# Conv 3x3 with 2x2 max pooling on one core: six row sums read odd rows from PSUM, head casts on another engine, and a new hand-written order

## Chip, cores, metric

One core of a Trainium2 chip. The metric is device microseconds of one execution. The kernel before took 104.8 us (median of 3 runs, 104.37 to 104.86).

## The reference

A batch of 16 images, 64 channels, 64x64, is convolved with 128 filters of 3x3 (padding 1), and each 2x2 block of the result is reduced to its maximum. The innermost lines are

```python
conv[b, co] += weight[co, ci, kh, kw] * x_pad[b, ci, kh:kh+h, kw:kw+w]
output[b, c, i, j] = np.max(conv[b, c, i*2:(i+1)*2, j*2:(j+1)*2])
```

with inputs and output in float32.

## The kernel before

**Tiles.** Two images stand on the 128 partitions (2 x 64 channels). Each pair of images is cut into four chunks of 16 input rows, which makes 8 x 4 = 32 steps, numbered 0 to 31. A step computes 8 pooled rows of two images. Index h (0 or 1) is the image: it uses rows 0 to 63 or 64 to 127 of TensorE, and matmuls of the two halves are issued in turn so that they run side by side. `lanes` (L251 to L259) holds products of h = 0 and h = 1 back until it has one of each, and then issues their three taps alternately; `product` is called once for each half.

**Two kinds of steps.** For a pair of output rows y0, y1 the kernel never needs the rows themselves, only their maximum, and that allows fewer products. In a K step (11 of 32) four products, PA1, PA2 (into a tile called `ta`) and PB1, PB2 (into `tb`), make y0 and y1 less a common part; the common part is PR, a product on the row sum `ks` of even and odd rows. The order is: `EV` copies `ta` to SBUF on ScalarE (L399), `MX` takes the maximum of `tb` and that copy on VectorE (L427), and PR is then added on TensorE. In a W step (21 of 32) the operands are made from the input in float32: the difference `we` of even and odd rows (step E), the differences `wd` of rows two apart (step D), and the sum `ws` of even and odd rows (step WS). P2 (on we) and P0 (on wd) go into `ta`; `SE` copies `ta` into `tb` on ScalarE (L411), P3 is added there, `EV` copies minus `ta` to SBUF (L401), `MX` takes the maximum, and P1 (on ws) is added at the end. In both kinds `OD` then copies the odd columns to SBUF on ScalarE (L431), and `CM` takes the maximum of even and odd columns on VectorE into an output tile (L437), which is stored by SyncE (SP) when both halves are done; the last step is stored half by half from the ScalarE queue and SP.

**Where the operands are made.** All E and D run on GpSimd (L332, L341) but for the E steps in `DIFF_ON_VECTOR`. A row sum WS runs on VectorE, as a plain sum of two SBUF operands (L323), or, for the steps in `SUM_BY_REDUCTION`, as a reduction over a doubled axis (L315). `on_vector` and `on_gpsimd` (L73 to L79) make a GpSimd instruction wait for the VectorE instruction marked last before it in the order; the reductions are not marked.

**PSUM.** There are eight accumulators of one bank each, handed out by the queue `free` (`take`, L222): every `ta`, every `tb` and every turned weight block takes one and gives it back.

**Head.** The weights are combined into seven blocks (D2, G0, D0, G2, GM, G1, GP): g0, g1 and g2 are casts on ScalarE (L461 to L463), D0, D2, GM and GP are made on VectorE, GS on GpSimd, u... copies one tap on GpSimd, T... turns a block on TensorE (L164), and V... (`turn_out`) copies it to `wt`. The first chunk of image pair 0 is loaded in two parts into `kfirst` and cast to bf16 in four pieces, XOa, XOb (odd rows) and XEa, XEb (even rows), on VectorE (L451). The second chunk goes to `ksecond` and is cast in two pieces, X1 and X2, on ScalarE (L458). Step 0 is multiplied in half products F.k.part (k: PA1, PA2, PB1, PB2), step 1 in G.k.part (k: P2, P0, P3), whose operands are made by Ea, Eb (VectorE) and Da, Db (GpSimd), with SEa and SEb as the halves of its seed.

**Loads.** W chunks go into three big tiles `wx` from SP (steps L and LB; LB waits for the marked VectorE instruction before it), later K chunks are cast by the GpSimd queue's DMA (LK, L95).

**Order.** Every engine works through its instructions in the order in which the string `ORDER` (L493 to L546) names the steps: one token is one call, `P2.4.1` being product P2 of step 4 for h = 1.

Of the kernel before, what the change touches and what calls it, by code (L numbers as in the profile page):

```python
# [11 lines left out]
def kernel(  # L12
# [169 lines left out]

# [126 lines left out]

    def ws(s):  # L310
# [17 lines left out]
    def we(s):  # L328
        row["we", s] = e_pool.tile([128, R, W], BF16, name="we")
        t, f = wx_rows(s)  # L330
        vector = s in DIFF_ON_VECTOR
        inst = (nc.vector if vector else nc.gpsimd).tensor_tensor(  # L332
            out=row["we", s], in0=t[:, f : f + 2 * R : 2, :], in1=t[:, f + 1 : f + 2 * R : 2, :], op=SUB
        )
        (on_vector if vector else on_gpsimd)(inst)
# [57 lines left out]
    ev, od, ot, made = {}, {}, {}, {}  # L393
# [39 lines left out]
    def colmax(s, h):  # L433
# [5 lines left out]
        made[s] = made.get(s, 0) + 1  # L439
# [3 lines left out]
        if s == N - 1:  # L443
            store = nc.scalar if made[s] == 1 else nc.sync
            store.dma_start(out=dst[:, h : h + 1], in_=src[:, h : h + 1])
        elif made[s] == 2:
            nc.sync.dma_start(out=dst, in_=src)


    def cast_rows(lo, hi):  # L450
        on_vector(nc.vector.tensor_copy(out=kx[0][:, lo:hi:2, :], in_=kfirst[:, lo:hi:2, :]))  # L451

    def cast_more(first):
# [13 lines left out]
        "GM": lambda: on_vector(nc.vector.tensor_sub(out=slots(GM), in0=gsum, in1=g1)),  # L467
        "GP": lambda: on_vector(nc.vector.tensor_add(out=slots(GP), in0=gsum, in1=g1)),
        "XOa": lambda: cast_rows(1, kmid),
        "XOb": lambda: cast_rows(kmid, khi),  # L470
        "XEa": lambda: cast_rows(0, kmid),
        "XEb": lambda: cast_rows(kmid + 1, khi),
# [11 lines left out]
        "SE": seed, "EV": evac, "MX": rowmax, "OD": odd, "CM": colmax,  # L484
    }
# [4 lines left out]
    for m in PRODUCTS:  # L490
# [7 lines left out]
        OD.0.0 OD.0.1 EV.1.0 KS.2 E.3 CM.0.1 EV.1.1 P1.1.1 D.3 CM.0.0 PR.2.1 PB1.2.0 P2.3.0 MX.1.0 PB2.2.0  # L498
        EV.2.1 P1.3.1 SE.3.1 EV.2.0 WS.3 MX.1.1 P1.1.0 SE.3.0 P0.3.0 MX.2.0 MX.2.1 EV.3.1 PR.2.0 EV.3.0 D.4
        MX.3.1 OD.2.0 PA1.5.1 OD.1.0 E.4 PA1.5.0 PA2.5.0 P3.3.0 OD.1.1 OD.2.1 L.12 L.14 PA2.5.1 OD.3.1  # L500
        P2.4.1 CM.1.1 CM.2.0 P2.4.0 CM.1.0 PA1.7.1 D.6 EV.5.0 CM.3.1 CM.2.1 MX.3.0 PA2.7.1 PB1.5.1 SE.4.0
        PA1.7.0 PA2.7.0 EV.5.1 SE.4.1 EV.7.0 PB2.5.1 P0.4.1 P0.4.0 P2.6.1 KS.7 E.6 P3.4.1 WS.4 WS.6 P1.3.0
        EV.4.0 PR.5.1 KS.5 WS.8 EV.7.1 P0.6.1 PB1.5.0 PB1.7.0 PB2.5.0 PB2.7.0 L.16 P1.4.1 EV.4.1 MX.5.1
        P3.4.0 OD.3.0 SE.6.1 MX.5.0 LK.1.0 LK.1.1 CM.3.0 MX.4.1 P3.6.1 OD.5.1 PB1.7.1 MX.7.0 PB2.7.1 PR.5.0
        OD.5.0 P2.6.0 EV.6.1 E.8 PR.7.0 MX.4.0 OD.4.1 OD.7.0 CM.5.1 D.8 P1.4.0 SE.6.0 OD.4.0 CM.5.0 E.9
        MX.6.1 CM.7.0 CM.4.0 P1.6.1 P2.8.0 CM.4.1 D.9 P2.8.1 SE.8.0 P0.6.0 P2.9.1 MX.7.1 P3.6.0 OD.6.1
        EV.6.0 P0.8.0 L.17 P3.8.0 SE.8.1 CM.6.1 PR.7.1 EV.8.0 OD.7.1 P0.8.1 MX.6.0 SE.9.1 E.11 MX.8.0 P1.6.0
        D.11 CM.7.1 P2.9.0 OD.6.0 EV.8.1 CM.6.0 WS.9 P3.8.1 P1.8.0 P0.9.1 PA1.10.1 SE.9.0 P2.11.0 OD.8.0
        L.19 L.20 P3.9.1 PA2.10.1 KS.10 EV.9.1 SE.11.0 P0.9.0 CM.8.0 E.14 P2.11.1 MX.9.1 P3.9.0 MX.8.1
        P0.11.0 EV.9.0 EV.10.1 MX.9.0 P1.9.1 D.14 E.12 P1.8.1 PA1.10.0 P3.11.0 PA2.10.0 SE.11.1 OD.9.1  # L510
        P1.9.0 P2.14.0 WS.11 CM.9.1 P0.11.1 P3.11.1 EV.11.0 EV.11.1 OD.8.1 OD.9.0 EV.10.0 P1.11.0 PA1.13.0
        PA1.13.1 MX.11.0 MX.11.1 PA2.13.1 D.12 L.22 L.23 PA2.13.0 P2.12.0 CM.8.1 CM.9.0 D.16 P1.11.1 EV.13.1
        P2.12.1 OD.11.0 SE.14.0 OD.11.1 PB1.10.1 WS.14 P0.14.0 CM.11.0 PB2.10.1 P3.14.0 CM.11.1 L.24 P0.12.0
        SE.12.1 P0.12.1 SE.12.0 P3.12.1 P3.12.0 EV.14.0 PB1.10.0 P2.14.1 WS.12 PB2.10.0 EV.13.0 MX.10.1
        EV.12.1 MX.14.0 E.16 EV.12.0 MX.12.1 PR.10.1 P1.14.0 MX.12.0 SE.14.1 OD.10.1 P1.12.0 PB1.13.1
        PA1.18.0 KS.15 KS.13 CM.10.1 P0.14.1 MX.10.0 OD.14.0 P3.14.1 CM.14.0 EV.14.1 P1.12.1 PR.10.0
        PB2.13.1 WS.16 MX.13.1 PA2.18.0 PA1.15.1 PA2.15.1 PR.13.1 OD.10.0 MX.14.1 PB1.13.0 OD.12.1 EV.18.0
        LK.2.0 P1.14.1 PB2.13.0 P2.16.0 CM.10.0 L.25 PA1.15.0 OD.12.0 EV.15.1 OD.13.1 CM.12.1 PA2.15.0
# [75 lines left out]
```

## Time and profile before

| what | value |
|---|---|
| median of three runs | 104.8 us (104.37 to 104.86) |
| span of the profiled execution | 103.4 us, granted TensorE clock 0.997 |
| TensorE (PE) busy | 96.6 us, 93% of the span, 909 matmuls |
| VectorE (DVE) busy | 91.9 us, 89% |
| ScalarE (ACT) busy | 82.1 us, 79% |
| GpSimd (POOL) busy | 75.7 us, 73% |
| bytes read and written | 17.14 MB and 8.39 MB |

The profile cuts the span into 40 equal slices of 2.6 us; each digit is the busy share of a slice in tenths.

```profile
PE   6889899999999999999999999999999999999910
DVE  1389899999999999999999999999989996979960
ACT  4545988986789997993887898987899898698820
POOL 6046969773995899998999997959997919970000
DMA  2989999999899999999847997198699232006252
```

A busy TensorE is not necessarily one at its peak, since matmuls overlap; the distance from one start to the next tells more. The other three compute engines feed it (GpSimd, VectorE) and empty its banks (ScalarE, VectorE), and idle time of theirs costs nothing by itself. The span ends with the last store.

### The profile page before, as it was taken

To read this page: it belongs to the slowest core of one execution; us is meant where nothing else is said; L and a number is where in the kernel's file an instruction comes from. 1 tells how busy PE (TensorE), PEld (TensorE's weight loads), DVE (VectorE), ACT (ScalarE), POOL (GpSimd) and SP (SyncE) were. 2 spreads that over 40 slices of the span, in tenths; PEclk is the share of its full clock that TensorE was granted. 3 is DMA by queue.
4 is the path that set the end of the run, shared out by engine and by line. 5 is a ranking of instruction groups with operands and counts; after the bars stand their busy time and mean duration, and the time that the engine had idled before them with its cause. 6 is when DMAs were issued, how large, how long until landed. Compare 5 with 4: busy or idle time off the path is not lost.

```text
span 103.4 us, 2542 instructions
## 1 busy us (share of the span) xinstructions
PE 96.6 (93%) x909; PEld 60.1 (58%) x909; DVE 91.9 (89%) x179; ACT 82.1 (79%) x181; POOL 75.7 (73%) x65
## 2 busy tenths in 40 slices
PE   6889899999999999999999999999999999999910
PEld 2366544555865565577777774556645777776500
DVE  1389899999999999999999999999989996979960
ACT  4545988986789997993887898987899898698820
POOL 6046969773995899998999997959997919970000
PEclk9999999999999999999999999999999999999998
DMA  2989999999899999999847997198699232006252
GB/s 63 265 297 283 389 319 337 384 405 270 219 212 307 304 302 292 341 356 225 175 131 210 252 381 263 51 203 271 173 158 257 80 136 101 0 13 223 74 202 102
DMA packets 13341, 23.33 MB, mean 226 GB/s; under 512 B 1040, under 2 KB 9488, under 8 KB 13328
## 3 DMA queue, kind: packets, MB, share of 16 engines
q1 hardware_dynamic: 12320, 20.68, 61.1%
q0 software_dynamic: 864, 2.36, 13.9%
q8 instruction: 7, 0.11, 0.4%
q10 hardware_dynamic: 144, 0.13, 0.4%
q14 instruction: 6, 0.05, 0.2%
HBM read 17.14 MB, written 8.39 MB: 247 GB/s over the span
## 4 chain that ended last, share of the span: by engine, by line
PE 83%; DMA 6%; DVE 5%; SPq 1%; issue 1%; DVEq 0%
PE acc L200 83%; DMA wx<-in_x_dram 6%; DVE acc L427 2%; DVE o L437 2%; DVE we L353 1%; SPq L114 0%; SPq L113 0%; SPq L109 0%; DVE ks L301 0%; DVEq L589 0%; DVEq L437 0%
## 5 line engine op out<-in xcount | busy, mean ns | idle before, releaser
L200 PEld LDWEIGHTS <-wt 64*128 64x128 bf16 x876 | 57.7, 94 | 34.1 <-issue 1.6
L341 POOL TENSOR_TENSOR wd<-wx 128x1024 bf16<-128x1024 f32 x20 | 47.1, 2360 | 7.6 <-PE acc L200 2.9
L200 PE MATMUL acc<-kx,wt 64*128 64x504 bf16 (+6 forms) x288 | 50.1, 356 | 0.4 <-DVE wt L181 0.4
L200 PE MATMUL acc<-wd,wt 64*128 64x504 bf16 (+3 forms) x264 | 50.1, 367 | 0.0
L427 DVE TENSOR_TENSOR acc<-acc,ev 128x512 f32<-128x512 f32 x64 | 42.0, 693 | 0.9 <-ACT ev L401 0.3
L200 PE MATMUL acc<-we,wt 64*128 64x512 bf16 (+2 forms) x132 | 31.9, 367 | 0.0
L200 PE MATMUL acc<-ws,wt 64*128 64x504 bf16 (+1 forms) x126 | 28.7, 377 | 0.1
L401 ACT ACTIVATE ev<-acc 128x512 f32<-128x512 f32 x42 | 25.1, 608 | 2.7 <-PE acc L200 2.3
L431 ACT COPY od<-acc 128x256 f32<-128x256 f32 x64 | 22.6, 379 | 5.8 <-PE acc L200 5.2
L437 DVE TENSOR_TENSOR o<-acc,od 128x256 f32<-128x256 f32 x64 | 24.5, 416 | 2.1 <-ACT od L431 1.9
L411 ACT COPY acc<-acc 128x512 f32<-128x512 f32 x40 | 23.0, 581 | 3.0 <-PE acc L200 1.7
L332 POOL TENSOR_TENSOR we<-wx 128x512 bf16<-128x512 f32 x16 | 20.2, 1271 | 3.4 <-DVE ws L323 2.4
L200 PE MATMUL acc<-ks,wt 64*128 64x504 bf16 (+1 forms) x66 | 16.5, 377 | 0.4 <-DVE acc L427 0.4
L315 DVE TENSOR_REDUCE ws<-wx 128x512 bf16<-128x1024 f32 x11 | 13.5, 1230 | 0.0
L399 ACT COPY ev<-acc 128x512 f32<-128x512 f32 x22 | 12.9, 595 | 0.6 <-PE acc L200 0.5
L323 DVE TENSOR_TENSOR ws<-wx 128x512 bf16<-128x512 f32 x10 | 7.0, 720 | 0.0
L301 DVE TENSOR_TENSOR ks<-kx 128x512 bf16<-128x512 bf16 x11 | 4.6, 429 | 0.4 <-ACT kx L458 0.4
L551 PE MATMUL acc<-const-bfloat16-1.0 128*128 128x512 bf16 x8 | 3.3, 589 | 0.8 <-PEq L575 0.8
L95 POOL DMA_DIRECT2D kx<-in_x_dram x6 | 3.5, 587 | 0.7 <-DVE kx L451 0.7
L151 POOL COPY wq<-wq 128x64 bf16<-128x64 bf16 x3 | 0.9, 314 | 3.2 <-ACT wq L462 2.5
L465 DVE TENSOR_TENSOR wq<-wraw 128x192 bf16<-128x192 f32 x1 | 0.5, 498 | 2.6 <-DMA wraw<-in_weight_dram 2.6
L368 POOL TENSOR_TENSOR wd<-wx 128x512 bf16<-128x512 f32 x2 | 2.5, 1260 | 0.4 <-DVE we L353 0.4
(30 smaller groups left out, 22.7 us busy)
## 6 DMA issues: line engine op xcount, KB each, us to landing
out_dram<-o SPq DMA_DIRECT2D x31, 256.0 KB, 4.7
wx<-in_x_dram SPq DMA_DIRECT2D x10, 512.0 KB, 7.8
wx<-in_x_dram SPq DMA_DIRECT2D x5, 544.0 KB, 8.7
wx<-in_x_dram SPq DMA_DIRECT2D x5, 480.0 KB, 7.7
kx<-in_x_dram POOLq DMA_DIRECT2D x2, 528.0 KB, 8.5
ksecond<-in_x_dram SPq DMA_DIRECT2D x1, 512.0 KB, 8.0
kx<-in_x_dram POOLq DMA_DIRECT2D x2, 256.0 KB, 6.7
kx<-in_x_dram POOLq DMA_DIRECT2D x1, 496.0 KB, 13.1
```

The costliest lines, as they stand in the source:

```text
L200: nc.tensor.matmul(acc[t][:, i0:i1, o0:o1], wt[lo : lo + CI, tap_of(m0, kw, h), :], rows(lo, i0, i1, c0, c1), start=start and kw == 1, sto ...
L301: nc.vector.tensor_tensor(out=row["ks", s], in0=t[:, f : f + 2 * R : 2, :], in1=t[:, f + 1 : f + 2 * R : 2, :], op=ADD)
L315: nc.vector.tensor_reduce(out=row["ws", s], in_=t[:, f : f + 2 * R, :].rearrange("p (r two) w -> p r w two", two=2), axis=mybir.AxisListTy ...
L323: nc.vector.tensor_tensor(out=row["ws", s], in0=t[:, f : f + 2 * R : 2, :], in1=t[:, f + 1 : f + 2 * R : 2, :], op=ADD)
L332: inst = (nc.vector if vector else nc.gpsimd).tensor_tensor(out=row["we", s], in0=t[:, f : f + 2 * R : 2, :], in1=t[:, f + 1 : f + 2 * R : ...
L341: nc.gpsimd.tensor_tensor(out=row["wd", s], in0=t[:, f + 1 : f + 1 + 2 * R, :], in1=t[:, f - 1 : f - 1 + 2 * R, :], op=SUB)
L399: nc.scalar.copy(out=ev[s, h], in_=acc[t])
L401: nc.scalar.mul(ev[s, h], acc[t], -1.0)
L411: nc.scalar.copy(out=acc[t], in_=acc[ta[s, h]])
L427: nc.vector.tensor_tensor(out=t, in0=t, in1=ev[s, h], op=MAX)
L431: nc.scalar.copy(out=od[s, h], in_=acc[tb[s, h]][:, :, 1::2])
L437: nc.vector.tensor_tensor(out=ot[s][:, h], in0=acc[t][:, :, 0::2], in1=od[s, h], op=MAX)
```

## The change

Six of the 21 row sums (steps 6, 8, 9, 17, 20, 24) get a new step XC: ScalarE copies the chunk's odd rows from `wx` into a free PSUM bank, and VectorE adds the even rows in SBUF to it. Where the step's difference E is on VectorE too (6 and 8), it reads the same bank. The bank goes back to `free` after the last reader. These instructions are not marked with `on_vector`. The lists of steps are changed: E of 3, 6, 8 on VectorE (before 3, 4, 6, 11), eight reductions (before eleven). XEa, XEb and XOb move from VectorE to ScalarE; of the turned blocks ScalarE copies GM and G1 (before GM, G0, G2). The pools of SBUF buffers are larger. A store is a token of its own (ST), so that SP can issue it later than directly after its CM. `ORDER` is new in every line; the new options that are empty tuples do nothing.

```diff
-    DIFF_ON_VECTOR = (3, 4, 6, 11,)
+    DIFF_ON_VECTOR = (3, 6, 8,)
-    SUM_BY_REDUCTION = (1, 3, 9, 11, 12, 14, 16, 17, 19, 20, 22,)
+    SUM_BY_REDUCTION = (1, 3, 12, 14, 16, 22, 28, 31,)
+    ODD_ROWS_IN_PSUM = (6, 8, 9, 17, 20, 24,)
+    TURNED_BY_SCALAR = ("GM", "G1",)
+    CAST_BY_SCALAR = ("XEa", "XEb", "XOb",)
...
-    d_pool = ctx.enter_context(tc.tile_pool(name="d_pool", bufs=5))
-    e_pool = ctx.enter_context(tc.tile_pool(name="e_pool", bufs=5))
-    ws_pool = ctx.enter_context(tc.tile_pool(name="ws_pool", bufs=5))
+    d_pool = ctx.enter_context(tc.tile_pool(name="d_pool", bufs=8))
+    e_pool = ctx.enter_context(tc.tile_pool(name="e_pool", bufs=7))
+    ws_pool = ctx.enter_context(tc.tile_pool(name="ws_pool", bufs=7))
...
-    ev_pool = ctx.enter_context(tc.tile_pool(name="ev_pool", bufs=7))
-    od_pool = ctx.enter_context(tc.tile_pool(name="od_pool", bufs=6))
-    o_pool = ctx.enter_context(tc.tile_pool(name="o_pool", bufs=6))
+    ev_pool = ctx.enter_context(tc.tile_pool(name="ev_pool", bufs=8))
+    od_pool = ctx.enter_context(tc.tile_pool(name="od_pool", bufs=8))
+    o_pool = ctx.enter_context(tc.tile_pool(name="o_pool", bufs=8))
...
+    def odd_rows(s):
+        t, f = wx_rows(s)
+        copied[s] = free.popleft()
+        users[s] = 2 if s in DIFF_ON_VECTOR else 1
+        nc.scalar.copy(out=acc[copied[s]], in_=t[:, f + 1 : f + 2 * R : 2, :])
+
+    def with_odd_rows(s, out, op):
+        t, f = wx_rows(s)
+        nc.vector.tensor_tensor(out=out, in0=t[:, f : f + 2 * R : 2, :], in1=acc[copied[s]], op=op)
+        users[s] -= 1
+        if users[s] == 0:
+            free.append(copied[s])
...
     def ws(s):
         row["ws", s] = ws_pool.tile([128, R, W], BF16, name="ws")
         t, f = wx_rows(s)
+        if s in ODD_ROWS_IN_PSUM:
+            with_odd_rows(s, row["ws", s], ADD)
+            return
...
-        made[s] = made.get(s, 0) + 1
+
+    def store(s, h=None):
         p, q = place[s]
         dst = out[2 * p : 2 * p + 2, :, q * R : (q + 1) * R, :].rearrange("b c h w -> c b (h w)")
         src = ot[s].rearrange("p b h w -> p b (h w)")
...
+        if h is None:
             nc.sync.dma_start(out=dst, in_=src)
+        else:
+            (nc.scalar, nc.sync)[h].dma_start(out=dst[:, h : h + 1], in_=src[:, h : h + 1])
...
+        "XC": odd_rows, "ST": store,
...
     ORDER = """
-        D0 g2 g1 TD0 TG2 g0 D2 XEa LB.3 LB.4 PR.0.1 TD2 VG2 PA1.2.1 VD0 TG0 uG1 TG1 GS F.2.0 VD2 XOa LB.6
-        LB.8 LB.9 GM VG0 F.3.0 XOb F.0.0 uGM F.1.0 VG1 F.0.1 TGM PA2.2.1 XEb LK.0.0 F.1.1 F.2.1 F.3.1 VGM GP
-        Ea KS.0 Eb EV.0.1 G.0.0 EV.0.0 G.0.1 uGP P2.3.1 SEa.0 SEa.1 SEb.1 MX.0.1 Da Db TGP SEb.0 MX.0.0 VGP
-        LK.0.1 X2 PR.0.0 G.1.0 X1 G.2.0 PB1.2.1 PB2.2.1 WS.1 G.2.1 G.1.1 L.11 P0.3.1 PA1.2.0 PA2.2.0 P3.3.1
+        g0 D2 D0 XOa g2 TD2 g1 TG0 XOb TD0 VD2 TG2 VG0 VD0 LB.3 GS GM F.0.0 uGM F.1.0 LB.9 XEb LB.4 LB.6 F.0.1
+        XEa GP F.1.1 uG1 F.2.0 EV.0.1 VG2 TGM KS.0 VGM uGP TG1 Ea F.3.0 EV.0.0 F.2.1 F.3.1 LK.0.0 VG1 G.0.0
+        SEa.0 SEa.1 Eb MX.0.1 TGP X1 G.0.1 X2 Da MX.0.0 LB.8 PR.0.1 VGP PR.0.0 PB1.2.0 PA1.2.0 SEb.0 Db WS.1
+        SEb.1 OD.0.1 OD.0.0 PA2.2.0 PA1.2.1 KS.2 CM.0.1 CM.0.0 G.1.0 E.3 G.1.1 EV.1.0 G.2.0 LK.0.1 L.11 P2.3.0
+        G.2.1 PA2.2.1 EV.1.1 MX.1.0 PB1.2.1 P2.3.1 EV.2.1 D.3 EV.2.0 MX.1.1 WS.3 L.17 PB2.2.0 PB2.2.1 SE.3.0
...
-        EV.31.1 P1.30.1 OD.29.1 P1.30.0 MX.31.1 OD.29.0 P1.31.1 CM.29.0 CM.29.1 P1.31.0 OD.30.1 CM.30.1
-        OD.30.0 OD.31.0 OD.31.1 CM.30.0 CM.31.0 CM.31.1
+        MX.30.1 P0.31.1 ST.25 P0.31.0 P3.31.1 ST.28 ST.26 P3.31.0 ST.21 EV.31.1 MX.29.0 P1.30.1 MX.31.1 ST.16
+        EV.31.0 OD.30.1 ST.27 MX.31.0 PR.29.1 PR.29.0 CM.30.1 P1.31.1 P1.31.0 ST.23 OD.29.0 CM.29.0 OD.29.1
+        OD.31.1 OD.31.0 CM.29.1 CM.31.1 CM.31.0 ST.30 ST.29 ST.31.1 ST.31.0
     """
```

Of the tokens in between, the prediction speaks of these, in the order in which they stand: after PR.2, the ScalarE queue has OD.2.1, XC.8, OD.3.0, SE.4.1; GpSimd has D.3, E.4, D.4, a kx load, D.6, a kx load, E.9, E.11, E.12, D.8, D.9, D.11, E.14, D.14, D.12, D.16; SP has LB.3, LB.9, LB.4, LB.6, LB.8, L.11, L.17, L.14, L.12, L.22, L.20, ST.2, L.25, L.16, L.23, ST.0.

More of the change, by code (lines that the diff above doesn't have):

```diff
@@ L331, in we @@
         vector = s in DIFF_ON_VECTOR
+        if vector and s in ODD_ROWS_IN_PSUM:
+            with_odd_rows(s, row["we", s], SUB)
+            return
         inst = (nc.vector if vector else nc.gpsimd).tensor_tensor(
@@ L442, in colmax, with cast_rows @@
         src = ot[s].rearrange("p b h w -> p b (h w)")
[L443 to L446, printed above, removed]
+        if h is None:
             nc.sync.dma_start(out=dst, in_=src)
-    def cast_rows(lo, hi):
-        on_vector(nc.vector.tensor_copy(out=kx[0][:, lo:hi:2, :], in_=kfirst[:, lo:hi:2, :]))
+        else:
+            (nc.scalar, nc.sync)[h].dma_start(out=dst[:, h : h + 1], in_=src[:, h : h + 1])
+    def cast_rows(n, lo, hi):
+        if n in CAST_BY_SCALAR:
+            nc.scalar.copy(out=kx[0][:, lo:hi:2, :], in_=kfirst[:, lo:hi:2, :])
+        else:
+            on_vector(nc.vector.tensor_copy(out=kx[0][:, lo:hi:2, :], in_=kfirst[:, lo:hi:2, :]))
     def cast_more(first):
@@ L466 @@
         "GS": lambda: on_gpsimd(nc.gpsimd.tensor_tensor(out=gsum, in0=g0, in1=g2, op=ADD)),
[L467 to L472, printed above, removed]
+        "GM": lambda: tap_sum("GM", GM, SUB),
+        "GP": lambda: tap_sum("GP", GP, ADD),
+        "XOa": lambda: cast_rows("XOa", 1, kmid),
+        "XOb": lambda: cast_rows("XOb", kmid, khi),
+        "XEa": lambda: cast_rows("XEa", 0, kmid),
+        "XEb": lambda: cast_rows("XEb", kmid + 1, khi),
         "X1": lambda: cast_more(0),
@@ L499 @@
[L499 to L518, printed above, removed]
```

104 lines of the change are left out of this document (68 added, 36 removed).

## The prediction

> **What bounds the kernel now.** I read the chain of waits first, then the timeline of the head and the tail, then the busy time by 5 us windows. The chain of waits (start, us, what) gives the shape of the whole:
>
> ```profile
> span 103.4 us, 2542 instructions
> 9.65 1.30 DVE acc L427 x2
> 10.99 64.95 PE acc L200 x609
> 75.96 20.42 PE acc L200 x186
> 97.73 1.74 DVE o L437 x5
> ```
>
> From 10.99 on, TensorE is the chain without a break worth naming: (64.95 + 20.42) us over 795 matmuls is 107.4 ns each. Two matmuls run side by side (the two 64-row halves), so a pair takes 0.215 us. The timeline of a quiet stretch shows one half starting at 92.31, 92.53 and 92.75, steps of 0.22: the body runs at its own pace. Taking 0.216 a pair, the starts of the trace lie later than that pace by about 0.5 us in sum between 13.02 and 97, the largest single gap 0.24 at 75.96. What a new order can win is there, in the head and in the tail:
>
> ```profile
> 9.65 1.28 DVE L427 TENSOR_TENSOR acc<-acc,ev 128x512 f32<-128x512 f32 x2
> 10.35 1.30 ACT L423 COPY acc<-acc 128x256 f32<-128x256 f32 x4 [0.47 <-ACT ev L399]
> 10.99 0.82 PE L200 MATMUL acc<-ks,wt 64*128 64x512 bf16 x6 [0.43 <-DVE acc L427]
> 11.54 1.15 ACT L458 CAST kx<-ksecond 128x512 bf16<-128x512 f32 x2
> 11.70 1.49 PE L200 MATMUL acc<-wd,wt 64*128 64x256 bf16 x24
> 13.02 1.25 PE L200 MATMUL acc<-kx,wt 64*128 64x512 bf16 x10
> ```
>
> At 10.99 the product PR.0 waited for the two row maxima MX.0 (DVE, 9.65 to 10.93); the matmuls that read the casts X1 and X2 (L458) come at 13.02, after the 24 of G.1 and G.2 on wd, so those casts hold nothing up.
>
> **The change, part by part.** Row prices:
>
> ```profile
> L315 DVE TENSOR_REDUCE ws<-wx 128x512 bf16<-128x1024 f32 x11 | 13.5, 1230 | 0.0
> L323 DVE TENSOR_TENSOR ws<-wx 128x512 bf16<-128x512 f32 x10 | 7.0, 720 | 0.0
> L427 DVE TENSOR_TENSOR acc<-acc,ev 128x512 f32<-128x512 f32 x64 | 42.0, 693 | 0.9 <-ACT ev L401 0.3
> L411 ACT COPY acc<-acc 128x512 f32<-128x512 f32 x40 | 23.0, 581 | 3.0 <-PE acc L200 1.7 <-DVE o L437 0.4
> L332 POOL TENSOR_TENSOR we<-wx 128x512 bf16<-128x512 f32 x16 | 20.2, 1271 | 3.4 <-DVE ws L323 2.4 <-DVE ks L301 0.5 <-PE acc L200 0.4
> ```
>
> *Sums and differences.* Reductions go from 11 to 8 (-3 x 1.230), plain sums from 10 to 7 (-3 x 0.720), differences on VectorE that read SBUF alone from 4 to 1 (-3 x 0.683, the by-shape row of L332 on DVE). Eight instructions (six sums, differences 6 and 8) now take one operand from PSUM. No row shows that form; below it lies 0.683 (both operands in SBUF), above it 0.725, the longest of L427, which also has one PSUM operand. I take L427's mean, 0.693: +5.5. VectorE also loses three casts (-1.0, L451) and gains one weight turn (+0.5, L181 at 0.41): -2.9 us in all. ScalarE gains six copies XC. Their price is unknown too: SBUF to PSUM lies between L411 (0.581) and the cast L458 (0.630). I take 0.581: +3.5. Three casts of 256 columns at 0.36 (L423's form) to 0.41 (L458's 0.630 less what 256 columns add between L423 and L411, 0.22) add 1.1 to 1.3, the turns -0.7: +4.0 in all. GpSimd gains one difference: +1.3. None of this is on the chain while TensorE is fed; if the cover goes, each microsecond late on ScalarE delays a seed (SE) and with it P3.
>
> *Head.* The first product needs XOa and the turned weights behind it on VectorE, which waited for kfirst until 5.48 as XEa did: start 6.2, as before. Then TensorE issues eight F products (seven of 0.33, one of 0.25) and two turns of 0.34, TGM and TG1. TG1 ran before 6.2 until now, so its 0.34 comes onto the path. That is 3.2: F ends at 9.45 (before: 9.26). XEa is third on ScalarE behind XOb and XEb: 6.3 (kfirst's second part landed 6.26) + 3 x 0.36 = 7.4, due at 7.45. MX.0.1 waits for the last F (0.27 long): 9.75, two maxima 1.28, PR.0 at 11.1 (before 10.99). PR.0 ends 11.75, and now the order puts PB1.2.0|PA1.2.1 next, which reads X1 and X2. On ScalarE these stand behind SEa.1, which ends about 10.7; they take 1.15. But ksecond was issued at 3.06 and took 8.0 to land:
>
> ```profile
> ksecond<-in_x_dram SPq DMA_DIRECT2D x1, 512.0 KB, 8.0
> ```
>
> So X2 ends between 11.85 (landed by 10.7) and 12.2 (landed 11.06). Behind X2 wait SEb.0 and SEb.1 (0.65), and G.1.0 waits for SEb.1, since it writes the bank that SEb reads: 12.55 to 12.9. Four G's of 0.33 end at 13.85 to 14.2. Before, the same work would have ended at 13.02 + 0.65 = 13.67. The head loses 0.2 to 0.55. The four wx loads that the order issued between 5.86 and 7.4 are now two, and the kx load on GpSimd's queue waits for Ea (9.1, was 8.28), so some of the landing's lateness should go; I take +0.4.
>
> The Trainium skill ("DMA: Bandwidth & Descriptors", Queues, rings and completion order) says that each DMA engine goes round between the queues that have work, packet by packet. By that rule the later kx load leaves ksecond the engines for longer, and the head would lose nearer 0.25; no run here shows it yet. The skill ("ScalarE: Activation LUTs", Rules for kernel authors) would leave plain arithmetic to VectorE, and the trace agrees for casts: 0.275 at best on DVE for 256 columns against the 0.36 to 0.41 above. By it XEa would be up to 0.1 late.
>
> *Start of the body.* SE.3.1 is next on that ScalarE chain: after OD.0 (0.66), EV.1 and EV.2 (about 0.54 each) and SE.3.0 it ends near 17.6, where P3.3.1 is due at 17.5: +0.1. GpSimd is fuller from there: D.3 starts at 14.75 (SEb.1 12.9, OD.0 0.66, CM.0.0 0.42, then E.3 0.69 on VectorE: 14.7, and D.3 waits for it), then E.4, D.4, two kx issues of 0.57, D.6, E.9, E.11, E.12, D.8: 4 x 2.36 + 4 x 1.27 + 1.14 = 15.7, so D.8 ends at 30.4. Counting pairs, P0.8 is due at 31.7; the others have at least as much room except D.3 (17.1 for 17.5). No loss. On SP the load L.25 waits for D.8 (30.4) to leave its rows, with L.16, L.23 and the store ST.0 behind it; D.16, the first heavy reader of L.16, starts on GpSimd no sooner than 41 (30.4 plus D.9, D.11, E.14, D.14, D.12), so a load issued at 31.4 that takes 8.7 has 1 us to spare. The column maximum of 9 waits for ST.0's buffer: about 32 plus 4.7 for the landing, due at 40.
>
> *Body.* Its 0.5 of small gaps may go or come again elsewhere: 0, bounds -0.5 and +0.6.
>
> *Tail.* Six column maxima followed the last row maximum:
>
> ```profile
> 97.73 2.07 DVE L437 TENSOR_TENSOR o<-acc,od 128x256 f32<-128x256 f32 x6
> 98.52 0.65 ACT L431 COPY od<-acc 128x256 f32<-128x256 f32 x2 [0.17 <-PE acc L200]
> 99.83 0.34 SPq L445 DMA_DIRECT2D out_dram<-o  x1
> ```
>
> Now five follow, so the end is set by ScalarE's last copy instead: 99.17 + 0.42 = 99.6 against 99.80: -0.2. The stores held back (16, 21, 23) stand behind ST.28 on SP, whose data are ready some 9 us before the end; 256 KB each after that is little beside a DMA share of 0.22 in 90 to 95. They cost nothing; if they were still moving at 99, the last store would land later than its 2.4.
>
> *Sum.* +0.4 + 0.1 + 0 - 0.2 = +0.3 on a span of 103.4: 103.7. The median of the three runs is 104.8, 1.4 above the span; I keep that difference: **105.1 us**.
>
> **Rivals.** *A, faster: the gaps go.* VectorE was busy 5.00 of 5.00 in most windows from 35 to 60, and gets 2.9 us of air; its sums no longer hold GpSimd (2.4 us of L332's idle time was for a plain sum). If the 0.5 in the body and the 0.22 before the last product go and ksecond lands by 10.7: +0.2 - 0.5 - 0.2 - 0.2 = -0.7: 104.1. Against it: those gaps are single ones with different releasers, and ScalarE has less air than before.
>
> *B, slower: a copy XC blocks ScalarE.* XC.8 waits on ScalarE for the load of chunk 8, now fifth among the wx loads and issued near 9.5. The fifth landed at 20.2 before, but the one issued at 8.59 needed 12.2 from the end of its issue, so 20.2 to 21.7. Behind XC.8 stand OD.3.0 and SE.4.1, and P3.4.1 is due at 22.6: 22.6 - 0.58 - 0.38 - 0.58 = 21.0. Up to that landing it costs nothing, from there it goes one to one into TensorE: up to 0.7, and with ksecond at 11.06 (+0.15) that is 105.9. For it: the DMA share is 1.05 in 10 to 20. Against: the bytes ahead of the load are no more than before.
>
> *C, no effect:* the sums from PSUM cost as much as they save (0.69 plus 0.58 elsewhere against 1.23) and the order only swaps small gaps; that ends at 104.8 and is counted with the forecast.
>
> **How the numbers follow.** Forecast with C 0.40, A 0.28, B 0.32. About 0.5%, 0.52 us, is what a measurement of this kernel can tell from no change: 104.3 to 105.3. Of the forecast 0.33 lie within and 0.07 above; of A 0.25 below and 0.03 within; of B 0.29 above and 0.03 within. Faster 0.25, same 0.39, slower 0.36. The forecast's own range is 104.7 to 105.5; to reach the other cases it is 103.9 to 106.2.
>
> **What would show it.** Head: PR.0 starting near 11.1, a gap on TensorE ended by ScalarE (the cast of ksecond, L501) at about 12, and the body's first full-width run near 14. Were there no such gap, the head step is wrong. B: a wait of ScalarE's L335 for a wx load near 20 with a TensorE gap behind it. A: no gaps over 0.05 between 20 and 97. Tail: last store issued within 1.5 of the last matmul. A gap behind GpSimd's wd (L381) anywhere, or stores moving past 99, would make the forecast wrong.

## The result and the profile after

The change took 106.03 us (median of 6 executions, 105.19 to 108.29), the kernel before 104.6 beside it; the ratio is 1.011, with a 95% interval of 1.0065 to 1.0157. A second set, run unedited as the first experiment, gave 105.64 and a ratio of 1.0092 (1.0057 to 1.0128). Medians and ranges here take every execution; a ratio leaves out those over 1.5% above the shortest of their kernel (that of 108.29, and two of the second set), though their granted clock was as high as that of the others (0.998 in that of 108.29). So the change costs about 1 us, and it widens the spread: the eight executions of the second set lie between 105.29 and 107.2, the nineteen of the kernel before beside them between 104.33 and 105.31.

The profile of the change that came with the result shows the execution of 108.29 us, the longest of the six; that of the second set shows one of 105.62. Both are read below, since what differs between two executions of one program is half of the answer. The page of the longer one, with the slices and the groups that answer to those of before (out<-in, count | busy us, mean ns of one | idle time before, and what ended it):

```profile
span 106.5 us, 2536 instructions
PE   7969999679999999799999999999999999999910
DVE  1398999739999996999999999986998898999950
ACT  4558888379788999779869789989799899798720
POOL 6056879609799987497999982999994999661000
DMA  3898999998899999979899979502910082006962
...
L467 DVE TENSOR_TENSOR acc<-acc,ev 128x512 f32<-128x512 f32 x64 | 42.1, 693 | 1.9 <-PE acc L219 1.1
L352 DVE TENSOR_REDUCE ws<-wx 128x512 bf16<-128x1024 f32 x8 | 9.8, 1227 | 0.0
L335 ACT COPY acc<-wx 128x512 f32<-128x512 f32 x6 | 3.6, 607 | 2.5 <-DMA wx<-in_x_dram 2.5
L360 DVE TENSOR_TENSOR ws<-wx 128x512 bf16<-128x512 f32 x7 | 4.7, 682 | 0.0
L339 DVE TENSOR_TENSOR ws<-wx,acc 128x512 bf16<-128x512 f32 x6 | 4.1, 680 | 0.0
```

The engines did what the change says: reductions fell to eight, the copies (L335) cost 0.607 us each and the sums from PSUM (L339) 0.680. TensorE's row now has a 6 and a 7 in slices 8 and 9 (19 to 24 us) and a 7 in slice 17 (43 to 45), where before it had nothing but 9 between the head and the end. One group shows why: of the six copies, one waited 2.5 us for a load. The chain of waits of the same execution (start, us, what):

```profile
9.11 12.90 DMA wx<-in_x_dram
...
22.08 0.07 ACT acc L335
...
22.61 0.38 ACT od L471
...
23.48 7.56 PE acc L219 x67
31.04 2.33 POOL wd L381
...
34.74 7.95 DMA out_dram<-o
...
44.80 55.30 PE acc L219 x510
```

Before, this chain was TensorE from 10.99 to 97. Now two transfers stand in it: the load of chunk 8, which the copy XC.8 waits for, and the store ST.0, for whose buffer a column maximum (L477) waits. Between them lies GpSimd's difference D.8 (L381), because the load L.25, ahead of ST.0 on SP's queue, waits for it. From 44.80 on TensorE again runs alone up to the last row maximum.

To compare executions whose first loads land at different times I take the stretch from the start of the first product to the end of the last one in each timeline. Before it is 92.46 us (6.22 to 98.68). In the change it is 95.51 in the long execution and 93.53 (5.42 to 98.95) in the ordinary one: +1.07, beside a loss in the medians of 1.43 in the first set and 0.91 in the second. Where the starts of TensorE's products lie later than its pace of 0.216 us a pair, on the half that waits longest:

| gap ends at (us, ordinary execution) | size | same place, long execution | what ends it |
|---|---|---|---|
| 16.5 to 20 | 0 | 1.16 | kx load of step 5 (landed 19.88 there) |
| 21.04, 24.43 | 0.44, 0.16 | 0.95, 0.16 | load of chunk 8, through XC.8 |
| 30.95 to 32.38 | 0.3 | 0.3 | GpSimd's D.8, ends 30.90; the last 0.13, at 32.38, a column maximum |
| 40.49, 42.03 | 0.34, 0.31 | 0.67, 0.31 | ST.0's landing, through a column maximum |
| 98.12 | 0.49 | 0.49 | last row maximum MX.31.0 |

The gaps of the ordinary execution add up to 2.0 us. The kernel before has 0.5 in its body and, by the same measure, 0.37 before its last product; that leaves 1.2 of the 2.0 for the 1.07. The first row of the table stands in the long execution alone.

### The profile page after: what moved, and what is told of

Read it like the earlier page. It is cut to its first block, busy times and chain, and to the rows that moved or that the text cites. A ratio compares the mean times of both kernels' runs of the same rounds, so it can differ in the third digit from the quotient of the medians.

```text
span 106.5 us, 2536 instructions
## 1 busy us (share of the span) xinstructions
PE 97.2 (91%) x909; PEld 61.0 (57%) x910; DVE 90.4 (85%) x176; ACT 85.2 (80%) x189; POOL 76.8 (72%) x66
## 4 chain that ended last, share of the span: by engine, by line
PE 60%; DMA 24%; DVE 6%; POOL 2%; issue 2%; SPq 1%; ACT 1%; DVEq 0%; ACTq 0%
PE acc L219 60%; DMA wx<-in_x_dram 12%; DMA out_dram<-o 7%; DMA kfirst<-in_x_dram 4%; POOL wd L381 2%; DVE o L477 1%; DVE acc L467 1%; DVE wt L188 1%; SPq L112 1%; ACT od L471 1%; DVE we L393 1%; DVE ws L360 1%; DVE wq L200 0%; DVE ks L320 0%; SPq L115 0%
## 5 line engine op out<-in xcount | busy, mean ns | idle before, releaser
L219 PEld LDWEIGHTS <-wt 64*128 64x128 bf16 x876 | 58.4, 94 | 36.6 <-issue 3.5
L381 POOL TENSOR_TENSOR wd<-wx 128x1024 bf16<-128x1024 f32 x20 | 46.9, 2356 | 12.8 <-DVE ws L360 7.5
L219 PE MATMUL acc<-wd,wt 64*128 64x504 bf16 (+3 forms) x264 | 51.9, 367 | 0.0
L219 PE MATMUL acc<-kx,wt 64*128 64x504 bf16 (+6 forms) x288 | 48.2, 356 | 3.1 <-DVE o L477 1.3
L219 PE MATMUL acc<-ws,wt 64*128 64x504 bf16 (+1 forms) x126 | 30.9, 377 | 0.3 <-DVE acc L467 0.2
L219 PE MATMUL acc<-we,wt 64*128 64x512 bf16 (+3 forms) x132 | 30.5, 367 | 0.0
L477 DVE TENSOR_TENSOR o<-acc,od 128x256 f32<-128x256 f32 x64 | 24.9, 417 | 6.2 <-ACT od L471 4.5
L372 POOL TENSOR_TENSOR we<-wx 128x512 bf16<-128x512 f32 x17 | 21.3, 1268 | 1.0 <-DVE ws L360 0.6
L219 PE MATMUL acc<-ks,wt 64*128 64x504 bf16 (+1 forms) x66 | 13.2, 377 | 0.0
L352 DVE TENSOR_REDUCE ws<-wx 128x512 bf16<-128x1024 f32 x8 | 9.8, 1227 | 0.0
L335 ACT COPY acc<-wx 128x512 f32<-128x512 f32 x6 | 3.6, 607 | 2.5 <-DMA wx<-in_x_dram 2.5
L360 DVE TENSOR_TENSOR ws<-wx 128x512 bf16<-128x512 f32 x7 | 4.7, 682 | 0.0
L339 DVE TENSOR_TENSOR ws<-wx,acc 128x512 bf16<-128x512 f32 x6 | 4.1, 680 | 0.0
## 6 DMA issues: line engine op xcount, KB each, us to landing
wx<-in_x_dram SPq DMA_DIRECT2D x10, 512.0 KB, 10.7
```

The lines of the kernel that those rows point to most:

```text
L219: nc.tensor.matmul(acc[t][:, i0:i1, o0:o1], wt[lo : lo + CI, tap_of(m0, kw, h), :], rows(lo, i0, i1, c0, c1), start=start and kw == 1, sto ...
L352: nc.vector.tensor_reduce(out=row["ws", s], in_=t[:, f : f + 2 * R, :].rearrange("p (r two) w -> p r w two", two=2), axis=mybir.AxisListTy ...
L360: nc.vector.tensor_tensor(out=row["ws", s], in0=t[:, f : f + 2 * R : 2, :], in1=t[:, f + 1 : f + 2 * R : 2, :], op=ADD)
L372: inst = (nc.vector if vector else nc.gpsimd).tensor_tensor(out=row["we", s], in0=t[:, f : f + 2 * R : 2, :], in1=t[:, f + 1 : f + 2 * R : ...
L381: nc.gpsimd.tensor_tensor(out=row["wd", s], in0=t[:, f + 1 : f + 1 + 2 * R, :], in1=t[:, f - 1 : f - 1 + 2 * R, :], op=SUB)
L477: nc.vector.tensor_tensor(out=ot[s][:, h], in0=acc[t][:, :, 0::2], in1=od[s, h], op=MAX)
```

## The experiments

Two theories were set against each other. *Queues*: the loss is made of waits for transfers between 19 and 45 us, which vary with each execution. *Steady*: it is made by the copies themselves, by ScalarE's 3 us of added work and by PSUM banks that they hold, and is the same in every execution.

**The change once more.** No edit.

> The changed kernel once more, nothing edited. Theory Q (queues): what it lost are waits for transfers between 19 and 45 us (the kx load that PA1.5 reads, the wx load that XC.8 copies, the store whose buffer CM.9 takes), and since landings differ from one execution to the next, so does its time: ratio 1.005 to 1.016, an execution near 103.5 us of span should show these gaps in TensorE short, a longer one should show them long. Theory S (steady): the loss comes from more work on ScalarE and from PSUM banks held by the copies; then the gaps stand in the same places with the same lengths in every execution, and few of them end at a landing.

Measured: 105.64 us, ratio 1.0092 (1.0057 to 1.0128). Two stretches of its timeline (start, us, what, and in brackets the idle time before and its releaser):

```profile
19.63 0.59 ACT L335 COPY acc<-wx 128x512 f32<-128x512 f32 x1 [0.78 <-DMA wx<-in_x_dram]
20.16 0.37 ACT L471 COPY od<-acc 128x256 f32<-128x256 f32 x1
20.56 0.42 DVE L477 TENSOR_TENSOR o<-acc,od 128x256 f32<-128x256 f32 x1 [0.62 <-ACT od L471]
21.04 0.37 PE L219 MATMUL acc<-kx,wt 64*128 64x512 bf16 x1 [0.21 <-DVE o L477]
...
40.01 0.42 DVE L477 TENSOR_TENSOR o<-acc,od 128x256 f32<-128x256 f32 x1 [0.89 <-DMA out_dram<-o]
40.49 0.81 PE L219 MATMUL acc<-kx,wt 64*128 64x512 bf16 x6 [0.16 <-DVE o L477]
```

Read the first four lines downwards: the copy starts when chunk 8 has landed (19.56); OD.3.0 stands behind it on ScalarE's queue, CM.3.0 needs that, and TensorE's next product needs the bank that CM.3.0 gives back. The pieces of the table that vary are waits for transfers; the 0.3 near 31 and the 0.49 at the end (0.12 more than before) do not vary.

**The load of chunk 9 behind that of chunk 8.** The change issues chunk 9 second among the big loads, though its sum is made much later.

```diff
- uGM F.1.0 LB.9 XEb LB.4
+ uGM F.1.0 XEb LB.4
- MX.0.0 LB.8 PR.0.1
+ MX.0.0 LB.8 LB.9 PR.0.1
```

> The load of chunk 9 goes back behind the loads of 4, 6 and 8 (before it stood second). Theory Q: the load of chunk 8 lands 1.5 to 2.5 us sooner, about 19.5 to 20.5, XC.8 no longer holds ScalarE, the gap near 23 (0.95 us in the profile of the change) goes; 0.5 to 1.0 us faster than the changed kernel, ratio to before 1.000 to 1.007. Theory S: the load order does nothing, ratio stays at 1.011.

Measured: 106.09 us, 1.0103 (1.0054 to 1.0151), no gain. Chunk 8 landed at 18.11, and the gaps at 21 and 24 were gone; but chunk 12, the last of that group of loads, landed at 28.82 (26.96 in the ordinary execution of the change). GpSimd's part of the timeline:

```profile
28.95 1.27 POOL L372 TENSOR_TENSOR we<-wx 128x512 bf16<-128x512 f32 x1 [1.92 <-DMA wx<-in_x_dram]
30.19 4.65 POOL L381 TENSOR_TENSOR wd<-wx 128x1024 bf16<-128x1024 f32 x2
```

E.12 waited 1.92 us, and D.8 and D.9 stood behind it; D.8 ended 1.3 us later than in the unedited execution, counted from the first product (26.7 for 25.5), and TensorE had a gap of 1.99 at 32.58. That the edit made chunk 12 late is not shown: without it the chunk landed at 29.48 in the long execution, and in a run below that keeps the loads of the change (one reduction less) at 29.64, where E.12 waited too. Only half of the question was answered: the wait for chunk 8 can be removed, and another one then decides.

**The first kx load earlier.** LK.0.0 moved from behind F.3.1 to directly behind uG1.

> The first kx load on GpSimd's queue is issued behind GP instead of behind Ea, about 1 us sooner. Theory Q: it lands about 1 us or more sooner than 19.9, and the gap at 19.9 before PA1.5 (1.16 us) shrinks by as much; part of it returns in the gap near 23, since that one waits for another landing: 0.2 to 1.0 us faster than the changed kernel. Theory S: no change.

Measured: 106.22 us median of 12, 1.0082 (1.0041 to 1.0122), between 104.81 and 107.25. Chunk 8 landed at 19.85, the gap at 21.33 was 0.33, that of ST.0 at 40.53 was 0.09, with the 0.31 behind it unchanged. By the medians the ratio is 1.014. The kx load cost nothing in this profile, and it had cost nothing in the ordinary execution of the change either, so this run does not tell the theories apart.

**Every store directly behind its second column maximum, as before.** The stores that the order holds back were put where the code of before issued them.

> Each store is issued directly behind the column maximum of its second half, as before the change; the loads keep their order among themselves. Theory Q: no CM waits for a landing near 42.7, the gaps at 43.3 and 44.8 (1.0 us together) go, but the stores now stand before loads on SP, so the loads from L.22 on come later: between 1.0 us faster and 0.5 us slower than the changed kernel, and the earlier gaps at 19.9 and 23.5 stay. Theory S: no change.

Measured: 120.51 us, 1.151 (1.147 to 1.156). SP's part of the timeline, and then the chain of waits, at the worst place:

```profile
58.87 8.76 SPq L485 DMA_DIRECT2D out_dram<-o  x5
67.68 1.47 SPq L112 DMA_DIRECT2D wx<-in_x_dram  x3
```

```profile
68.27 8.77 DMA wx<-in_x_dram
...
77.06 0.07 DVE ws L360
```

In this trace SP worked its queue in order: from 58.87 to 67.63 it issued five stores, each held until its data were ready, and the three loads behind them could start only then; a row sum waited for one of them until 77.06. Not all of the 15.8 us is waiting: behind each of the two longest gaps of TensorE (5.49 at 36.56, 6.90 at 78.42) its granted clock was about half (0.54 in 36.6 to 41.0, 0.56 in 78.5 to 82.0), and pairs started 0.43 apart until 40.7 and 81.8, which by my estimate costs 3.5 us against the pace of 0.216. This order needs its late stores: they can't be undone alone.

**No copies.** The six XC steps are left out; sums 9, 17 and 20 are reductions, the others plain.

```diff
- SUM_BY_REDUCTION = (1, 3, 12, 14, 16, 22, 28, 31,)
- ODD_ROWS_IN_PSUM = (6, 8, 9, 17, 20, 24,)
+ SUM_BY_REDUCTION = (1, 3, 9, 12, 14, 16, 17, 20, 22, 28, 31,)
+ ODD_ROWS_IN_PSUM = ()
```

> The changed order with no copy XC at all: sums 9, 17, 20 are reductions again, 6, 8, 24 plain sums, differences 6 and 8 read SBUF on VectorE. Theory Q (waits for transfers decide): only the part goes that hangs on XC.8 (0.6 us of gaps at 21.0 and 24.4 in the run of the unedited kernel), the others stay (31 to 32.4: 0.3, 40.5 to 42: 0.65, 98.1: 0.5): about 0.6 us faster than the changed kernel, ratio to before 1.002 to 1.006. Theory S (copies and ScalarE's load decide): nearly all 1.0 us goes, ratio 1.000 or below. If the reductions and plain sums make VectorE late: slower than the changed kernel.

Measured: 109.35 us, 1.043 (1.038 to 1.048), 3.7 slower than with the copies. Two parts of the timeline, VectorE's (start 23.45) and GpSimd's (23.02):

```profile
23.45 2.85 DVE L372 TENSOR_TENSOR we<-wx 128x512 bf16<-128x512 f32 x1
...
23.02 2.72 POOL L381 TENSOR_TENSOR wd<-wx 128x1024 bf16<-128x1024 f32 x1 [2.42 <-DVE we L372]
```

A difference of 0.68 us took 2.85: it could not go on until GpSimd's difference of rows two apart was through (25.74). That is what the copies buy, besides sums at 0.68 for reductions at 1.23: with one operand in PSUM the same work runs at 0.68 beside GpSimd. Differences and plain sums of two SBUF operands do not. How the 3.7 us divides between the two was not tried.

**Three copies in the order of before.** Steps 9, 19 and 22 get a copy in place of a reduction, all else is as before.

```diff
- ... EV.8.1 ...  EV.21.1 ...  CM.15.0 ...
+ ... EV.8.1 XC.9 ...  EV.21.1 XC.19 ...  CM.15.0 XC.22 ...
```

> The kernel before, its order and lists kept, with three copies put in where a bank was free: sums 9, 19 and 22 are made from PSUM in place of reductions; each copy stands 3 to 9 tokens ahead of its sum. Theory Q: the copies by themselves cost nothing, ratio 0.997 to 1.003. Theory S: 3 x 0.58 on ScalarE and the banks they hold show up as gaps, ratio 1.004 or more.

Measured: 107.3 us, 1.0245 (1.0196 to 1.0294): 0.8 us a copy. From its table of waits between 30 and 67 us (engine, line, waited for: us, times, longest):

```profile
DVE ws L339 <- ACT acc L335: 1.2, 2, 0.7
...
ACT acc L451 <- DVE ws L339: 0.8, 1, 0.8
PE acc L219 <- ACT acc L451: 0.8, 1, 0.8
```

The new dependence runs both ways. VectorE waits for the copy, and a seed on ScalarE waits for the bank that the sum still reads; the gap on TensorE at 62.91 is 1.01. Where the order makes no room for it a copy is dear, which speaks for the theory of steady costs, in this order.

**Two waits removed.** XC.8 behind EV.5.1, when the chunk is there, and ST.0 in front, behind ST.2.

> The changed kernel with two tokens moved: XC.8 stands behind EV.5.1 on ScalarE, so that OD.3.0 and SE.4.1 no longer wait for the load of chunk 8, and the store ST.0 is issued directly behind ST.2, ahead of the load that waits for D.8. Theory Q: the gaps at 21.0, 24.4 and 40.5 (0.94 us) go, the rest (0.3 at 31 to 32, 0.3 at 42, 0.5 at 98) stays: 0.5 to 0.9 us faster than the changed kernel, ratio 1.000 to 1.005. Theory S: no gain.

Measured: 106.22 us, 1.0123 (1.0062 to 1.0184). ScalarE no longer waited for the load, but VectorE waited 0.9 for the copy, and about 0.5 of gaps at 24 took the place of those at 21. The later place was too late; with it a flaw came into this run and the next.

**The two waits and the loads in the order of need.** As above, and the loads in the order 3, 4, 6, 8, 9, 11, 12, 14, 17, LK.0.0 early, E.12 behind D.9.

> The two moves of the run before, and the loads in the order in which they are needed: 3, 4, 6, 8, 9, 11, 12, 14, 17 (chunk 9 stood second, 17 ahead of 14 and 12), the first kx load 1 us sooner, and E.12 behind D.8 and D.9 on GpSimd. Theory Q: as two_waits in an execution where loads land early, and without the gaps of a late one (19.9, 23.5, 32.6): ratio 0.999 to 1.004 and a spread of the times like that of the kernel before (1 us). Theory S: no gain over the changed kernel.

Measured: 105.63 us, 1.0082 (1.0053 to 1.0111), with a narrower spread (105.33 to 106.31 in 12). No transfer stood in the chain of waits after the head; the gaps left were about 0.5 at 24 (made by the late XC.8), 0.3 at 27, 0.4 at 33 and 0.4 at 98.

**Loads in the order of need, XC.8 left where the change has it.**

```diff
- ... LB.3 ... LB.9 ... LB.4 LB.6 ... LB.8 ... L.11 ... L.17 ... L.14 ... L.12 ...
+ ... LB.3 ... LB.4 LB.6 ... LB.8 LB.9 ... L.11 ... L.12 ... L.14 L.17 ...
- F.2.1 F.3.1 LK.0.0
+ uG1 LK.0.0 F.2.0
- E.11 PR.5.0 E.12 ... D.9
+ E.11 PR.5.0 ... D.9 E.12
- P0.11.0 ST.0
+ ST.2 ST.0
```

> The run waits_and_loads without its move of the copy of chunk 8: loads of the wx chunks in the order of need, the first kx load two GpSimd instructions earlier, ST.0 directly behind ST.2, E.12 behind D.9; XC.8 stays where the change has it. Queues: with the chunk there in time and the copy early enough for VectorE, the body's gaps between 19 and 45 fall from 1.6 to 2 us to under 0.5, first product to last product under 92.4 us, median 105.0 to 105.3. Steady: the gap at 23.6 of waits_and_loads goes (0.46, made by that move), those near 27, 31 and 33 (0.1 to 0.4 each) stay, first to last product 92.5 to 92.8, median 105.3 to 105.6.

Measured: 105.42 us median of 12, ratio 1.0031 (1.0006 to 1.0056). Chunk 8 landed at 18.01, and TensorE had no gap over 0.06 from 12 to 32; of the 0.44 and 0.16 of the change, and of the 0.3 to 0.4 that stayed near 27 in the last two runs, nothing was left. A gap of 0.25 at 32.48, ended by a column maximum, stayed. 92.82 us from first to last product. One wait for a store came back in this execution (0.56 at 36.29, where a column maximum waited 0.55). Two executions of the twelve took 106.61 and 107.42, so the spread did not narrow. About two thirds of the loss are gone by the ratios, half to two thirds by the medians (1.0045 here), with all six copies in place; what was moved are issues and one GpSimd instruction, E.12. D.8 now ended 23.6 us after the first product and not 25.5: of these 1.9 us 1.27 are E.12, which no longer stands ahead of it.

**One reduction less before the end.** VectorE has hardly any idle time from 90 us to the last row maximum, so I took its last reduction, that of step 31, as a plain sum.

```diff
- SUM_BY_REDUCTION = (1, 3, 12, 14, 16, 22, 28, 31,)
+ SUM_BY_REDUCTION = (1, 3, 12, 14, 16, 22, 28,)
```

> The change with one row sum, that of step 31, as a plain sum (0.68) in place of a reduction (1.23). VectorE had no idle time from 90 to 98.07 in the second execution of the change, and the last product waited 0.49 us for its last row maximum. If the reduction is the cause of that gap, the gap falls to under 0.1 and the median by 0.4 to 0.5 against the unedited change, to about 105.2. If something else ends it (the copy EV.31 on ScalarE, which waited 0.77 us for TensorE before it), the gap stays at 0.3 or more and the median within 0.15 of 105.6.

Measured: 107.11 us (105.74 to 110.83 in 6), 1.0172 (1.012 to 1.0223), gap before the last product 0.51. Up to 92 us this program is the change, so its execution is one more sample of that: 0.85 at 22.05 for chunk 8, and 1.57 at 33.40, where E.12 waited 1.4 for chunk 12. The edit itself had no effect for a reason that the next run's profile shows too.

**Both together.** loads_only and the plain sum of step 31.

> Both edits together: loads_only and sum31_plain. Queues: the gains add, since one lies in 19 to 45 us and the other at 98: span 102.7 to 103.0, median 104.4 to 104.8, at or below the kernel before. Steady: 0.5 us of small gaps between 24 and 34 remain, median 105.0 to 105.2.

Measured: 105.19 us median of 12, ratio 1.0036 (1.0001 to 1.0072). Its profiled execution, 104.96 us, took 92.36 from first to last product, as before (92.46). The gap before the last product stayed at 0.51. VectorE's line of the timeline, then GpSimd's:

```profile
92.16 1.45 DVE L360 TENSOR_TENSOR ws<-wx 128x512 bf16<-128x512 f32 x1
...
90.70 2.36 POOL L381 TENSOR_TENSOR wd<-wx 128x1024 bf16<-128x1024 f32 x1 [1.82 <-DVE ws L360]
```

The plain sum took 1.45 and not 0.68, since GpSimd's D.31 was running until 93.06: longer than the reduction of 1.23 that it replaced. So this edit tests nothing of the gap.

**As the last, without the copy of chunk 8.** Its sum and its difference on VectorE read SBUF.

> As loads_sum31, and chunk 8 is not copied to PSUM: its sum and its difference on VectorE read SBUF, ScalarE has one copy of 0.61 us less at 20 us, and one bank is free there. Steady: the gaps between 21 and 34 shrink by 0.2 to 0.4 against loads_sum31, and so does the median. Queues: no difference beyond 0.1, since the chunk lands in time.

Measured: 105.87 us median of 8, 1.0096 (1.0059 to 1.0133): about 0.6% slower than with the copy (the two intervals just overlap), the opposite of what steady costs would give; the queues had expected no difference. First the same stretch with the copy, then without it; in each VectorE's lines and then GpSimd's:

```profile
21.64 0.68 DVE L339 TENSOR_TENSOR we<-wx,acc 128x512 bf16<-128x512 f32 x1
22.24 0.68 DVE L339 TENSOR_TENSOR ws<-wx,acc 128x512 bf16<-128x512 f32 x1
...
24.03 0.68 DVE L360 TENSOR_TENSOR ws<-wx 128x512 bf16<-128x512 f32 x1
...
21.36 2.36 POOL L381 TENSOR_TENSOR wd<-wx 128x1024 bf16<-128x1024 f32 x1 [1.13 <-DVE ks L320]
```

```profile
21.64 0.68 DVE L372 TENSOR_TENSOR we<-wx 128x512 bf16<-128x512 f32 x1
22.24 0.69 DVE L360 TENSOR_TENSOR ws<-wx 128x512 bf16<-128x512 f32 x1
...
24.04 1.66 DVE L360 TENSOR_TENSOR ws<-wx 128x512 bf16<-128x512 f32 x1
...
22.42 2.73 POOL L381 TENSOR_TENSOR wd<-wx 128x1024 bf16<-128x1024 f32 x1 [2.19 <-DVE we L372]
```

The wait of GpSimd for E.8 (2.19) is the mark that the code puts on differences and sums of SBUF operands. D.6 started 1.06 later for it and ended at 25.15, and so ran into the next plain sum, which took 1.66. VectorE was 1 us late, and TensorE had gaps of 0.50 and 0.15 near 27 and 0.46 in sum near 33. With the copy the gaps near 27 do not exist, and 0.3 is left near 32. The run takes away the copy and adds two marked instructions, so it prices the two together.

So most of the body's loss is that of the queues: it goes when issues (and E.12) are moved, with all six copies in place. In this order the copy of chunk 8 has no net cost that shows, though in that of before three copies have one; the other five were not taken away singly. Steady are the gap at the end and 0.25 to 0.3 near 32, behind a column maximum. No version beat the kernel before; the best two, at 1.003 and 1.004, come within half a per cent of it.

## Why the prediction was right or wrong

The time lies in the range (103.9 to 106.2) and on the slower side, to which 0.36 was given, but 0.9 above the 105.1 of the likeliest case. What happened in every execution looked at is rival B's mechanism (0.60 us in the ordinary one), and with it a store of the same kind (0.65) and a late difference of GpSimd (0.2), for which the prediction's sum had nothing; a late kx load came on top in the long one. Point by point:

- *What bounds the kernel* held: TensorE at 0.216 a pair, 0.5 of small gaps in the body. VectorE's air could win no more than that, and rival A came in part, behind the losses: from the start of the 401st matmul of the products to that of the 801st (of 876) the ordinary execution took 43.1 us and the kernel before 43.5; more than half of the difference is the 0.24 at 75.96, which is gone.
- *Sums and differences.* The instructions' durations, added up from the traces, fell by 3.1 us on VectorE (predicted 2.9) and rose by 4.3 on ScalarE (4.0) and by the one difference on GpSimd (1.27 for 1.3). The busy time of the pages, which counts the overlap of two instructions once, shows less of it: 1.5, 3.1 and 1.1. The unknown form cost 0.680, below the bound of 0.683 and not at L427's 0.693; the copy 0.607, between 0.581 and 0.630, not at the lower end taken. "None of this is on the chain while TensorE is fed" was right. What was not seen is a merit of the form that the experiments show: it runs beside GpSimd.
- *Head*, +0.4, was wrong. The term failed at ksecond's landing, taken as 10.7 to 11.06. It landed at 8.78 and 9.35 in the two executions of the change, and at 9.75 with the order of before (the run with three copies): 11.07 was this one execution. X1 and X2 ran from 10.44, no gap was ended by L501, and PR.0 started 4.73 after the first product, before 4.77. The head is equal. The timeline of the change's head:

```profile
10.44 1.14 ACT L501 CAST kx<-ksecond 128x512 bf16<-128x512 f32 x2
10.94 0.82 PE L219 MATMUL acc<-ks,wt 64*128 64x512 bf16 x6
11.48 0.64 ACT L463 COPY acc<-acc 128x256 f32<-128x256 f32 x2
11.63 0.82 PE L219 MATMUL acc<-kx,wt 64*128 64x512 bf16 x6
```

- *Start of the body*, "No loss", is the step that failed most. Counted from the first product, GpSimd's D.8 ended at 25.5 (30.90 with a first product at 5.42), not at 24.2 (30.4 with 6.2), and the due time, 25.5, was right: TensorE waited for it, the gap behind wd that the prediction named as a sign against itself. D.3 even began 0.76 earlier than the sum has it. But the sum of 15.7 lays GpSimd's instructions end to end, and in the ordinary execution the engine stood idle 1.77 in front of D.6, until the row sum KS.7 was made on VectorE, and 0.56 in front of E.9, until WS.4 was. Without the wait for chunk 8 (loads_only) 1.1 and 0.6 of this are still there, so the term was short by itself and the load made it worse. GpSimd's timeline of the ordinary execution:

```profile
21.41 2.36 POOL L381 TENSOR_TENSOR wd<-wx 128x1024 bf16<-128x1024 f32 x1 [1.77 <-DVE ks L320]
...
24.85 3.73 POOL L372 TENSOR_TENSOR we<-wx 128x512 bf16<-128x512 f32 x3 [0.56 <-DVE ws L360]
```

  The column maximum that needs ST.0's buffer was put at "about 32 plus 4.7, due at 40". Its due time was right too (33.7 after the first product, 33.8 in the prediction). But ST.0 stands behind L.25, which waits for D.8, and so was issued 1.2 later than counted, at 32.40; and it landed at 39.92, 7.5 after the start of its issue and 7.0 after its end, in the long execution at 42.69. The landing of 4.7 is the median of all stores of before; the longest there took 8.8 from the start of its issue. This place cost 0.65 in the ordinary execution (0.34 and the 0.31 behind it), and the prediction's sum had nothing for it.
- *Rival B* had the right place and order of queueing, but its point was too late. It took SE.4.1 as the first to be missed, at a landing of 21.0, that is 14.8 us after the first product. OD.3.0 is missed earlier, by way of CM.3.0 and the bank. Landing less the gap that followed, counted from the first product, gives the point in four executions of this order: 13.7 (landed 19.56, gap 0.44, first product 5.42), 13.7 (19.85, 0.33, 5.85), 13.9 (20.57, 0.85, 5.87) and 13.7 in the long one, with its earlier gap of 1.16 taken off. With loads in the order of need and XC.8 in its place (loads_only, loads_sum31) chunk 8 landed 11.9 and 11.1 after the first product, and there was no gap. So the load was late in every execution of the change that was looked at in this order, not only in some.
- *Rival C*, that copies cost what they save, fell: taking one away cost about 0.6%, taking all away 3.4% (1.0432 for 1.0092), in both with what takes their place, and adding three where there was no room cost 2.45%.
- *Tail*, -0.2, did not come: the last store was issued 1.23 after the end of the last product (98.95 to 100.18), before it was 1.15 (98.68 to 99.83). Five column maxima follow the last row maximum, as predicted, and ScalarE's last copy sets the end; but that copy ended 0.68 after the last product and not 0.49, the time of before that the prediction kept. Before, the two halves of the last product ended 0.2 apart, and the copy of the first could start at 98.52; now both end within 0.02, and it starts at 98.98. The last product also came 0.12 later behind its row maximum: the half that waits longest waited 0.49, before 0.37 (the prediction's 0.22 is the other half, which is now 0.33). In the timeline of the longer execution:

```profile
97.53 3.31 DVE L467 TENSOR_TENSOR acc<-acc,ev 128x512 f32<-128x512 f32 x5
98.83 1.08 ACT L441 ACTIVATE ev<-acc 128x512 f32<-128x512 f32 x2 [0.77 <-PE acc L219]
100.90 0.82 PE L219 MATMUL acc<-ws,wt 64*128 64x512 bf16 x6 [0.16 <-DVE acc L467]
```

  Between the third and the fourth of the five maxima VectorE waited 0.07 us, and the trace gives TensorE as the releaser: the fourth, MX.31.1, reads the bank of P3.31.1, whose end TensorE signalled at 99.45. So a VectorE with less to do would have won nothing here. The last two maxima took until 100.84, the product was due at 100.41, and the order has too few products left behind P3.31 to cover them; one with more was not tried.
- *Sum.* 1.4 us was kept between the span and the time. In the runs it is 1.8 for the kernel before (104.66 for a span of 102.9) and for the change, so the profiled execution of before was itself a late one, by 0.4. A due time read from one execution carries such a shift with it.

What remains open: why the best version still has a median 0.2% above before while its profiled execution is as short from first to last product (neither profile is of the median execution: that of loads_sum31 lies 0.23 under its median, that of before 0.4 over).

What the prediction took from the Trainium skill on the queues ("DMA: Bandwidth & Descriptors", Queues, rings and completion order) can't be told from chance here: ksecond landed earlier, but it did so with the order of before too. Another page bears on the experiments. The Trainium skill ("SBUF — State Buffer", Who interferes with whom) says that a VectorE instruction with two SBUF inputs and a GpSimd instruction that reads SBUF exclude each other for the whole of the first one, and that one SBUF input does not contend. The traces agree: the plain sum at 24.04 ended 0.55 us after D.6, that at 92.16 ended 0.55 after D.31, so nearly all of their 0.68 lay behind it; and with the copies in place the eight instructions with a PSUM operand took 0.677 to 0.689 each, three of them wholly beside D.6.

## What to carry to other kernels

An instruction that is moved to another engine takes its waits with it: the copy made ScalarE, which in the body had read no input before, wait in order for a load, and everything behind it in the queue paid. When a change moves work in front of a transfer, find the first instruction behind it whose result TensorE needs, count the due time from there, and put the loads in the order in which they are needed before anything else is judged. Work out such margins from several executions: counted from the first product, chunk 8 landed 14.0 to 15.8 us behind it in the four executions named above, where about 13.7 was due, and a margin of 3.3 us for ST.0 (36.7 for 40) was used up.

## What was not expected of the hardware

The load of chunk 8 landed at 19.56, 20.57 and 22.01 us in three executions with the order of the change (the second is sum31_plain, the same program up to 92 us), and the store ST.0 7.0 to 7.2 us after its issue where stores took 1.8 to 2.3 at the end of the run. A sum of one SBUF and one PSUM operand cost no more (0.680) than one of two SBUF operands (0.682), and of the two it alone kept that time beside GpSimd's differences of rows two apart (L381); the two-SBUF form took 1.45, 1.66 and 2.85. After TensorE had stood idle for 5 us and more (stores_at_once), its granted clock was half for about 4 and 3 us of work.
